# Dilated attention on one core: keys and values held whole, or loaded per pair of heads in a full-array layout

## The chip, the cores and the metric

The kernel runs on one core of one Trainium2 chip. The metric is the device time of one execution of the whole program, in microseconds (us). Times and traces come from the chip's own profiler.

## The reference

Two transformer blocks over 256 tokens of width 1024. The first block holds, in this order, feed-forward layers, a gated linear recurrence, shared keys and values, and a dilated attention. The part that the change touches is the last two:

```python
kv = (x @ kv_w).reshape(bsz, s, 2, N_HEADS, HEAD_DIM)      # 16 heads of 64
...
q = (x @ w_q).reshape(bsz, s, N_GROUPS, N_HEADS, HEAD_DIM) # three query groups
for g, (window, dilation) in enumerate(((128, 1), (512, 4), (2048, 16))):
    o, l = dilated_group(q[:, :, g], k, v, slopes, window, dilation)
...
wts = softmax(stack(lses), axis=0)
out = sum(wts[..., None] * stack(outs), axis=0)
return out.reshape(bsz, s, N_HEADS * HEAD_DIM) @ w_o
```

In `dilated_group` a query at t sees the keys t, t-d, t-2d, ... within its window, with a bias of minus slope times distance. Weighting three softmaxes by the softmax of their log-sum-exps is one softmax over the scores of the three groups side by side, and so the kernel computes it.

## The kernel before, in words

All large products are done in F32R, a float form with a shortened mantissa that TensorE takes in one pass. To keep accuracy each operand is split into a high and a low part, and three matmuls are summed (high by high, high by low, low by high; `mm3`). Weights stream from memory in units of eight 128x128 tiles: SyncE's queue brings a unit (`raw`), ScalarE rounds it to the high part (`whi`, L87), VectorE subtracts to get the low part (`wlo`, L99). `pump` keeps the splits up to six units ahead of use.

`kv` (the stage of shared keys and values) makes keys with features on partitions, two heads of 64 to a tile of 128, and writes their high and low parts to memory as `kh` and `kl`. Values have tokens on partitions and go to `vsc`, through `kt` (L634).

`attn` begins with seven loads on GpSimd's queue: the distance table `dt`, the scales `qs`, the keys `KH` (four loads, L653; each head's high part stands twice, in both halves of the partitions), `KL` (L654; low parts of two heads in the two halves), and the values `Vt` (L655). The queries are made by 24 tiles of matmuls in groups, `put` writes a head's high part into its own half of the partitions and the low part into the other half.

Heads go through a software pipeline, one `step` per head: `scores` of head i, `soft` of head i-1, `trans` of head i-2, `pv` of head i-3. The list `PLAN` says how many steps stand after each half group of query matmuls, `HOOKS` places the last ones amid the output projection's first wave. A scheduler then orders each engine's queue. In `scores` there are six products per head: for the later 128 queries and then for the earlier 128, each against the three groups. Each is two matmuls of 256 columns: the stacked high and low queries against KH (128 rows), and the high queries alone against KL (64 rows):

```python
self.mm(b[:, i], q[:, i % 3, c], KH[:, h, :], i % 2 == 0, False)
self.mm(b[:, i], q[r, i % 3, c], KL[r, pr, :], False, True)
```

VectorE adds the distances and takes the maximum in one instruction (L687 for the later queries, 768 columns, L690 for the earlier, 384), scales the maxima (`m`, L693), ScalarE takes exponentials with a running sum (L694, L695). In `soft` GpSimd adds two groups (L705), VectorE the third and the division (L706, L707). `trans` transposes on TensorE, ScalarE copies back (`pt`, L717). In `pv` the values of a head (64 columns of weights) are multiplied with `pt`; even heads fill the lower, odd heads the upper half of one PSUM bank's partitions. These products are in plain f32, which takes two instructions each in the trace.

Of the kernel before, what the change touches and what calls it, by code (L numbers as in the profile page):

```python
# [8 lines left out]
F32 = mybir.dt.float32  # L9
# [26 lines left out]
HOOKS = (1, 3, 5)  # L36
RAWS = 5
# [20 lines left out]
class Builder:  # L58
# [13 lines left out]
    # ---------------------------------------------------------------- weights  # L72
# [96 lines left out]
    # ---------------------------------------------------------------- layer norm  # L169
# [4 lines left out]
    def emb_begin(self):  # L174
        """The columns and the meta tokens that the norm of all tokens adds to the first block's last one."""
# [8 lines left out]
    def sums(self, m, N, off, sq, eng, eng2=None):  # L184
        """Running sums of x and x^2 over the feature tiles."""
# [32 lines left out]
    def prep(self, ms, ln, N, off, fold=True):  # L218
        """What the next norm needs of the feature tiles ms, which end together."""
# [24 lines left out]
    def scale_in(self, m, ln, N, off):  # L244
        """x <- x g, once the sums have what they need of it."""
# [9 lines left out]
    def stats(self, N, eps, tail=None, dst=None):  # L255
        """Mean and deviation of every token from the running sums; tail: the last tile's share comes on top."""
# [46 lines left out]
    def norm_last(self, ln, N, off, i, eng, rstd, nm):  # L303
        """Normalises a feature tile that scale_in has been over."""
# [17 lines left out]
    def filler(self, specs, ln, N, off, eps, pool, tag="fv", bufs=2, when=(1, 3)):  # L322
        """First output tiles of a stage, from the not yet normalised input."""
# [84 lines left out]
    def out_proj(self, K, hh, hl, spec, coef, ln, N, off, fold, waves, korder=None, hooks={}):  # L408
        """x <- x + coef * (h @ W), in waves of output tiles; hooks: what is emitted amid the first wave."""
# [22 lines left out]
    # ---------------------------------------------------------------- feed forward  # L432
# [26 lines left out]
    # ---------------------------------------------------------------- RG-LRU  # L459
# [142 lines left out]
    # ---------------------------------------------------------------- shared keys and values  # L602
    def kv(self, ln_in, eps):
        nc = self.nc
        N, off = SEQ, META
        with self.tc.tile_pool(name="kv", bufs=1) as p:
# [16 lines left out]
            for c in range(4):  # L623
# [9 lines left out]
                t = p.tile([128, 2, N], F32, tag="kt", name="kt", bufs=2)  # L633
                nc.scalar.copy(t, P)  # L634
                nc.scalar.dma_start(out=self.vsc[:, :, c * 256:(c + 1) * 256], in_=t)

    # ---------------------------------------------------------------- dilated attention
    def attn(self, ln_in, ln_out, eps):
        nc = self.nc
        N, off = SEQ, META  # L640
        with self.tc.tile_pool(name="attn", bufs=1) as p:
            KH = p.tile([128, N_HEADS, N], F32R, name="KH")
            KL = p.tile([128, 8, N], F32R, name="KL")
            Vt = p.tile([128, 2, D], F32, name="Vt")
# [17 lines left out]
            def put(pr, g, src):  # L662
                """High part of a head's queries in its own half of the partitions, low part in the other one."""
# [11 lines left out]
            def scores(h):  # L675
                e, pr = h % 2, h // 2
                q = Q[pr][e]
                r = slice(64 * e, 64 * e + 64)
                b = self.bank(3).rearrange("p a n -> p (a n)").rearrange("p (g n) -> p g n", n=N)
# [762 lines left out]
```

## Time and profile before

| | |
|---|---|
| median of 3 runs | 1812.07 us (1810.32 to 1812.13) |
| profiled execution, span from first to last instruction | 1813.3 us (the page gives no other time of its own) |
| TensorE (PE) busy | 1741.0 us, 96% |
| VectorE (DVE) busy | 1272.0 us, 70% |
| ScalarE (ACT) busy | 1032.6 us, 57% |
| GpSimd (POOL) busy | 230.0 us, 13% |
| mean granted TensorE clock | 0.970 |
| dilated attention, first score matmul to the end of the output projection's first wave | 772.3 to 938.3 us |

PE rows are matmuls, PEld rows the loads of their weights. A matmul's duration in a row includes the way through the array, so that neighbours overlap; what a matmul costs in a stream is the distance of its start from the next start. PEclk is the granted clock, as a share of 2.4 GHz.

### The profile page before, as it was taken

The page shows a single profiled execution, that of the slowest core. Times are in us where ns is not written, and L with a number is a line of the kernel's source. Part 1 is how long each engine was busy: PE and PEld are TensorE (multiplying, and loading weights), DVE is VectorE, ACT ScalarE, POOL GpSimd, SP SyncE. Part 2 cuts the span into 40 slices and gives each one's busy share as a digit, 9 for nine tenths or more (in the row PEclk, how much of TensorE's full clock was granted, in tenths as well). Part 3 has the DMA queues.
Part 4 walks back from the last instruction along what each step waited for, and adds up shares of the span by engine and source line. Part 5 has one row for each costly group of instructions (what it writes and reads, how often), then busy time and mean ns, then how long its engine had stood idle before and what let it go on. Part 6 is the DMA issues. An engine that isn't in the chain of part 4 may idle for free.

```text
span 1813.3 us, 34554 instructions
## 1 busy us (share of the span) xinstructions
PE 1741.0 (96%) x13558; PEld 1675.4 (92%) x13558; DVE 1272.0 (70%) x2399; ACT 1032.6 (57%) x2090; POOL 230.0 (13%) x266
## 2 busy tenths in 40 slices
PE   8999978999999999999999999799999999999997
PEld 8999977999999999977789999788999998899996
DVE  6666899966676666756668666897965569687653
ACT  6444666744465444644547445775744457575443
POOL 0001355000100001201120001320200030120001
PEclk9999988999999999968999999999999999999999
DMA  8555435565548555732225555433365554246550
GB/s 292 185 187 186 145 105 168 170 209 186 182 156 280 186 187 186 208 118 82 82 85 179 188 183 184 154 106 106 118 208 176 177 188 152 83 129 223 186 186 35
DMA packets 85372, 296.80 MB, mean 164 GB/s; under 512 B 10892, under 2 KB 14232, under 8 KB 84696
## 3 DMA queue, kind: packets, MB, share of 16 engines
q1 hardware_dynamic: 80216, 283.79, 47.1%
q0 software_dynamic: 1424, 7.38, 1.3%
q10 hardware_dynamic: 3568, 3.41, 0.6%
q8 instruction: 106, 1.74, 0.4%
q14 instruction: 58, 0.48, 0.1%
HBM read 290.24 MB, written 4.19 MB: 162 GB/s over the span
## 4 chain that ended last, share of the span: by engine, by line
PE 82%; DVE 11%; ACT 3%; issue 2%; DMA 1%; POOL 1%; DVEq 0%; SPq 0%; POOLq 0%; ACTq 0%
PE ps L147 81%; DVE wlo L99 3%; DMA KL<-kl 1%; PE ps L155 1%; ACT whi L87 1%; DVE uc L510 0%; DVE gl L300 0%; DVE T L561 0%; DVE xf L252 0%; POOL wlo L99 0%; DVE nt L291 0%; DVE gl L215 0%; POOL acc L193 0%; DVE rstd L277 0%; DMA raw<-in_wst_dram 0%
## 5 line engine op out<-in xcount | busy, mean ns | idle before, releaser
L87 ACT CAST whi<-raw 128x512 fp32r<-128x512 f32 x1074 | 615.5, 617 | 525.7 <-issue 311.0
L99 DVE TENSOR_TENSOR wlo<-raw,whi 128x512 fp32r<-128x512 f32 x1032 | 685.7, 701 | 321.5 <-ACT whi L87 319.6
L147 PE MATMUL ps<-gh,whi 128*128 128x256 f32 (+3 forms) x2864 | 829.0, 290 | 19.6 <-ACT gh L297 8.7
L147 PE MATMUL ps<-gl,whi 128*128 128x256 f32 (+3 forms) x2864 | 823.3, 288 | 1.0 <-DVE gl L300 1.0
L147 PE MATMUL ps<-gh,wlo 128*128 128x256 f32 (+3 forms) x2864 | 818.4, 286 | 0.0
L147 PEld LDWEIGHTS ps<-gh,whi 128*128 128x128 f32 x2864 | 549.3, 192 | 27.2 <-ACT gh L297 9.3
L147 PEld LDWEIGHTS ps<-gl,whi 128*128 128x128 f32 x2864 | 550.9, 192 | 5.9 <-issue 2.6
L147 PEld LDWEIGHTS ps<-gh,wlo 128*128 128x128 f32 x2864 | 551.1, 192 | 1.3 <-issue 0.7
L147 PE MATMUL ps<-hh,wlo 128*128 128x256 f32 (+1 forms) x1056 | 298.0, 282 | 0.0
L147 PE MATMUL ps<-hh,whi 128*128 128x256 f32 (+1 forms) x1056 | 297.9, 282 | 0.0
L147 PE MATMUL ps<-hl,whi 128*128 128x256 f32 (+1 forms) x1056 | 297.7, 282 | 0.0
L147 PEld LDWEIGHTS ps<-hl,whi 128*128 128x128 f32 x1056 | 199.0, 188 | 0.0
L147 PEld LDWEIGHTS ps<-hh,whi 128*128 128x128 f32 x1056 | 199.0, 188 | 0.0
L147 PEld LDWEIGHTS ps<-hh,wlo 128*128 128x128 f32 x1056 | 198.8, 188 | 0.0
L193 POOL TENSOR_TENSOR acc<-xf 128x256 f32<-128x256 f32 (+1 forms) x10 | 7.6, 759 | 1060.7 <-DVE xf L252 907.7
L443 DVE TENSOR_TENSOR th<-th,ps 128x512 f32<-128x512 f32 (+1 forms) x62 | 42.9, 691 | 54.3 <-PE ps L147 54.3
L193 POOL TENSOR_TENSOR acc<-acc,xf 128x256 f32<-128x256 f32 (+1 forms) x50 | 45.5, 910 | 192.3 <-DVE xf L252 177.3
L99 POOL TENSOR_TENSOR wlo<-raw,whi 128x512 fp32r<-128x512 f32 x42 | 63.3, 1536 | 46.2 <-ACT whi L87 46.2
L252 DVE SCALAR_TENSOR_TENSOR xf<-ps,xf 128x256 f32<-128x256 f32 (+1 forms) x80 | 32.9, 422 | 41.1 <-PE ps L147 40.9
L198 ACT ACTIVATE sq<-xf 128x256 f32<-128x256 f32 (+1 forms) x88 | 35.6, 410 | 44.6 <-DVE xf L252 36.8
L211 ACT ACTIVATE gh<-xf,prm 128x256 fp32r<-128x256 f32 (+1 forms) x64 | 32.1, 508 | 47.9 <-DVE xf L252 47.9
L215 DVE SCALAR_TENSOR_TENSOR gl<-xf,prm,gh 128x256 fp32r<-128x256 f32 (+1 forms) x64 | 44.5, 706 | 11.0 <-ACT gh L211 11.0
(330 smaller groups left out, 1927.8 us busy)
## 6 DMA issues: line engine op xcount, KB each, us to landing
raw<-in_wst_dram SPq DMA_DIRECT2D x537, 512.0 KB, 3.4
cst<-in_c_mix_dram POOLq DMA_DIRECT2D x2, 1138.0 KB, 5.5
KH<-kh POOLq DMA_DIRECT2D x4, 512.0 KB, 13.7
kh<-kh ACTq DMA_DIRECT2D x4, 256.0 KB, 4.8
kl<-kl ACTq DMA_DIRECT2D x4, 256.0 KB, 6.6
vsc<-kt ACTq DMA_DIRECT2D x4, 256.0 KB, 6.0
KL<-kl POOLq DMA_DIRECT2D x1, 1024.0 KB, 21.5
Vt<-vsc POOLq DMA_DIRECT2D x1, 1024.0 KB, 23.9
```

The lines of the kernel that those rows point to most:

```text
L87: self.nc.scalar.copy(hi[:, q:q + 512], self.raws[u][:, q:q + 512])
L99: eng.tensor_tensor(lo[:, q:q + 512], r[:, q:q + 512], h[:, q:q + 512], op=ALU.subtract)
L147: self.nc.tensor.matmul(out, lhsT, rhs, start=start, stop=stop, skip_group_check=True)
L155: self.nc.tensor.matmul(out, in_, self.ident[0:n, 0:n], start=True, stop=True, is_transpose=True, skip_group_check=True)
L193: eng.tensor_tensor(a[:, 0, 0:N], x0, x, op=ALU.add)
L198: self.nc.scalar.activation(sq[:, 0:N], self.xf[:, m, off:off + N], AF.Square)
L211: return self.nc.scalar.activation(self.gh[:, m, c], self.xf[:, m, off:off + N], AF.Copy, scale=g)
L215: return self.nc.vector.scalar_tensor_tensor(self.gl[:, m, c], self.xf[:, m, off:off + N], g, self.gh[:, m, c].bitcast(F32), op0=ALU.mult, ...
L252: self.nc.vector.scalar_tensor_tensor(x, banks[m][:, 0:N], coef, x, op0=ALU.mult, op1=ALU.add)
L443: nc.vector.tensor_tensor(th, th, pu, op=ALU.mult)
```

## The change

Keys go to memory as one array `khl` with high and low parts side by side, values as `vsc` with each head's 64 columns inside 128, the other 64 zero (two `kt` buffers zeroed once by GpSimd, filled by four small copies per 256 columns). Attention loads keys and values per pair of heads into five rotating buffers (`KVB`), the first pair before the table, the last three pairs as buffers come free. Both score matmuls of a product now contract over 128 rows: against high parts that stand in both halves, and against low parts that stand in both halves (so that low by low is added too). The earlier queries take 128 columns of keys in place of 256, and lie without gaps in PSUM. The slope is folded into the reduction (minimum in place of maximum), and the scaling of `m` goes. In `pv` both heads of a pair are summed into the whole bank, each with zeros in the other's half.

```diff
+KVB = 5
 def kv(self, ln_in, eps):
             def put(c2, src):
-                h = p.tile([128, 2, N], F32R, tag="kh", name="kh", bufs=2)
-                lo = p.tile([128, 2, N], F32R, tag="kl", name="kl", bufs=2)
-                self.split(h, lo, src)
-                nc.scalar.dma_start(out=self.kh[:, 2 * c2:2 * c2 + 2, :], in_=h.bitcast(F32))
-                nc.scalar.dma_start(out=self.kl[:, 2 * c2:2 * c2 + 2, :], in_=lo.bitcast(F32))
+                h = p.tile([128, 2, 2, N], F32R, tag="kh", name="kh", bufs=2)
+                self.split(h[:, :, 0], h[:, :, 1], src)
+                nc.scalar.dma_start(out=self.khl[:, 2 * c2:2 * c2 + 2], in_=h.bitcast(F32))
...
+            KT = [p.tile([128, 2, 2, 2, 128], F32, name="kt") for _ in range(2)]
+            for t in KT:
+                nc.gpsimd.memset(t, 0.0)
...
-                t = p.tile([128, 2, N], F32, tag="kt", name="kt", bufs=2)
-                nc.scalar.copy(t, P)
-                nc.scalar.dma_start(out=self.vsc[:, :, c * 256:(c + 1) * 256], in_=t)
+                t = KT[c % 2]
+                P = P.rearrange("p t (a e d) -> p a t e d", a=2, e=2)
+                for i in range(2):
+                    for e in range(2):
+                        nc.scalar.copy(t[:, i, :, e, 64 * e:64 * e + 64], P[:, i, :, e, :])
+                nc.scalar.dma_start(out=self.vsc[:, 2 * c:2 * c + 2], in_=t)
 def attn(self, ln_in, ln_out, eps):
+            def load(pr):
+                K = p.tile([128, 2, 2, N], F32R, tag="K", name="K", bufs=KVB)
+                W = p.tile([128, 2, 2, 128], F32, tag="W", name="W", bufs=KVB)
+                for e in range(2):
+                    for r in (0, 64):
+                        nc.gpsimd.dma_start(out=K[r:r + 64, e].bitcast(F32), in_=self.khl[64 * e:64 * e + 64, pr])
+                nc.gpsimd.dma_start(out=W, in_=self.vsc[:, pr])
+                KV[pr] = K, W
+            load(0)
...
-            for e in range(2):
-                for r in (0, 64):
-                    nc.gpsimd.dma_start(out=KH[r:r + 64, e::2, :].bitcast(F32), in_=self.kh[64 * e:64 * e + 64])
-            nc.gpsimd.dma_start(out=KL.bitcast(F32), in_=self.kl)
-            nc.gpsimd.dma_start(out=Vt, in_=self.vsc)
+            for pr in range(1, KVB):
+                load(pr)
...
                 for i in range(6):
-                    c = slice(128, 256) if i < 3 else slice(0, 128)
-                    self.mm(b[:, i], q[:, i % 3, c], KH[:, h, :], i % 2 == 0, False)
-                    self.mm(b[:, i], q[r, i % 3, c], KL[r, pr, :], False, True)
+                    c, n, o = (slice(128, 256), 256, i * 256) if i < 3 else (slice(0, 128), 128, 384 + i * 128)
+                    for t in range(2):
+                        self.mm(b[:, o:o + n], q[:, i % 3, c], K[:, e, t, 0:n], o % 512 == 0 and t == 0, t == 1)
...
-                nc.vector.tensor_scalar(m, m, -SLOPES[h], None, op0=ALU.mult)
...
             def pv(h):
-                self.mm(b[r:r + 64, 0:256], Vt[:, 0, h * 64:(h + 1) * 64], pt[:, 0:256], True, False)
-                self.mm(b[r:r + 64, 128:256], Vt[:, 1, h * 64:(h + 1) * 64], pt[:, 256:384], False, True)
-                if h % 2:
+                self.mm(b[:, 0:256], W[:, 0, e], pt[:, 0:256], e == 0, False)
+                self.mm(b[:, 128:256], W[:, 1, e], pt[:, 256:384], False, e == 1)
+                if e:
                     del self.held["o"]
-                    self.split(oh[:, h // 2], ol[:, h // 2], b[:, 0:256])
+                    self.split(oh[:, pr], ol[:, pr], b[:, 0:256])
+                    if pr + KVB < 8:
+                        load(pr + KVB)
```

The order of the queues moves with it. TensorE around the first score matmuls of a late head, before (`gh`, `gl` are the normalised input's parts, `q` the queries):

```order
L147 MATMUL ps<-KH,q 128x256
L147 MATMUL ps<-KL,q 128x256
L147 MATMUL ps<-KH,q 128x256
L147 MATMUL ps<-KL,q 128x256
L147 MATMUL ps<-gh,whi 128x256
L147 MATMUL ps<-gl,whi 128x256
L147 MATMUL ps<-gh,wlo 128x256
```

and a late head after the change, with the transposes of one head and the value products of another behind it:

```order
L148 MATMUL ps<-K,q 128x256 x6
L148 MATMUL ps<-K,q 128x128 x8
L148 MATMUL ps<-gh,whi 128x256
L156 MATMUL ps<-ident,t 128x128 x3
L148 MATMUL ps<-pt,W 128x256
L148 MATMUL ps<-pt,W 128x128
```

KH and KL no longer alternate, and half of the score matmuls have 128 columns. At the very start of attention's scores, 4 score matmuls, 4 weight matmuls, 4 score matmuls, 24 weight matmuls and 2 score matmuls stand ahead of the first reduction.

GpSimd's queue at the start of attention, before:

```order
L649 DMA dt<-in_c_dist_dram 128x1152
L650 DMA qs<-in_c_qs_dram 128x8
L653 DMA KH<-kh 64x8x256 x4
L654 DMA KL<-kl 128x2048
L655 DMA Vt<-vsc 128x2048
L705 TENSOR_TENSOR t<-s 128x256
L705 TENSOR_TENSOR t<-s 128x128
```

and after, from the last of the first five pairs on (`K` and `W` are a pair's keys and values):

```order
L657 DMA W<-vsc 128x512
L656 DMA K<-khl 64x512
L712 TENSOR_TENSOR t<-s 128x256
L656 DMA K<-khl 64x512
L712 TENSOR_TENSOR t<-s 128x128
L656 DMA K<-khl 64x512
L712 TENSOR_TENSOR t<-s 128x256
L712 TENSOR_TENSOR t<-s 128x128
L656 DMA K<-khl 64x512
```

The loads of the sixth pair stand between the additions of the first two heads; each waits until its part of a buffer has been read.

## Rows read from the trace of the kernel before

**Rows 1.** The page's shares of the span: engine, busy us, instructions.
```profile
PE 1741.0 (96%) x13558; PEld 1675.4 (92%) x13558; DVE 1272.0 (70%) x2399; ACT 1032.6 (57%) x2090; POOL 230.0 (13%) x266
```

**Rows 2.** Busy time by stretch: PE, PEld, DVE, ACT, POOL, granted clock, DMA.
```profile
772.30:938.30 166.00, 162.35 (x809) 124.79 (x808) 101.98 (x250) 77.77 (x167) 21.62 (x32) 0.85 0.26 86
```

**Rows 3.** TensorE's timeline at the full clock, then its weight loads: start, us, what.
```profile
902.64 0.28 PE L147 MATMUL ps<-gh,wlo 128*128 128x256 f32 x1
902.76 0.28 PE L147 MATMUL ps<-KH,q 128*128 128x256 f32 x1
902.97 0.38 PE L147 MATMUL ps<-KL,q 64*128 64x256 f32 x1
903.28 0.38 PE L147 MATMUL ps<-KH,q 128*128 128x256 f32 x1
...
902.64 0.19 PEld L147 LDWEIGHTS ps<-KH,q 128*128 128x128 f32 x1
902.97 0.18 PEld L147 LDWEIGHTS ps<-KL,q 64*128 64x128 f32 x1
```

**Rows 4.** TensorE's timeline at the lower clock level.
```profile
796.89 0.58 PE L147 MATMUL ps<-KL,q 64*128 64x256 f32 x1
797.40 0.58 PE L147 MATMUL ps<-gh,whi 128*128 128x256 f32 x1
797.77 0.41 PE L147 MATMUL ps<-gl,whi 128*128 128x256 f32 x1
797.99 0.41 PE L147 MATMUL ps<-gh,wlo 128*128 128x256 f32 x1
```

**Rows 5.** TensorE's waits in the stretch: us in total, times, longest.
```profile
PE ps L147 <- DMA KL<-kl: 3.6, 1, 3.6
```

**Rows 6.** Busy time by shorter stretches, columns as in rows 2.
```profile
778.30:801.50 23.20, 23.20 (x78) 17.30 (x78) 10.39 (x24) 7.73 (x18) 2.68 (x4) 0.57 0.19 67
...
808.00:828.00 20.00, 20.00 (x84) 16.18 (x83) 10.68 (x30) 7.69 (x18) 2.31 (x4) 0.66 0.17 54
```

**Rows 7.** Groups of instructions in the stretch: TensorE's score matmuls on KL.
```profile
L147 PE MATMUL ps<-KL,q 64*128 64x256 f32 x96 | 40.0, 417 | 3.6 <-DMA KL<-kl 3.6
```

**Rows 8.** TensorE's timeline in the second block: plain f32 products on the full array.
```profile
1243.21 0.41 PE L147 MATMUL ps<-Qr,Kr 128*128 128x128 f32 x2
1243.46 0.81 PE L147 MATMUL ps<-Vr,st 128*128 128x96 f32 x6
1244.10 0.84 PE L147 MATMUL ps<-Qr,Kr 128*128 128x256 f32 x4
1244.78 0.81 PE L147 MATMUL ps<-Vr,st 128*128 128x96 f32 x6
```

**Rows 9.** TensorE's timeline: the value products of one head, and what follows.
```profile
906.89 0.86 PE L147 MATMUL ps<-pt,Vt 128*64 128x256 f32 x4
907.69 0.38 PE L147 MATMUL ps<-gh,whi 128*128 128x256 f32 x1
```

**Rows 10.** Weight loads of 64 and of 128 columns: ns minimum, median, maximum.
```profile
L147 PEld LDWEIGHTS ps<-pt,Vt x64: 132/137/231, 809.3 to 935.8; 128*64 128x64 f32 x64
...
L147 PEld LDWEIGHTS ps<-Qr,Kr x32: 188/190/192, 1235.5 to 1570.2; 128*128 128x128 f32 x32
```

**Rows 11.** GpSimd's groups from 740 to 940: the issues of KH.
```profile
L653 POOL DMA_DIRECT2D KH<-kh x4 | 2.8, 695 | 0.0
```

**Rows 12.** VectorE's groups in the stretch: the scaling of m.
```profile
L693 DVE TENSOR_SCALAR m<-m 128x2 f32<-128x2 f32 x16 | 2.6, 164 | 0.2
```

**Rows 13.** The tile kt in the keys-and-values stage: ns minimum, median, maximum.
```profile
L634 ACT COPY kt<-ps x4: 577/580/588, 550.7 to 563.6; 128x512 f32<-128x512 f32 x4
```

**Rows 14.** Busy time in the second block's two mixers, columns as in rows 2.
```profile
1190.00:1290.00 100.00, 93.35 (x656) 83.24 (x655) 82.93 (x216) 65.41 (x166) 23.95 (x32) 0.97 0.34 112
1495.00:1595.00 100.00, 96.03 (x703) 88.48 (x702) 79.81 (x209) 65.70 (x169) 10.83 (x21) 0.98 0.38 127
```

**Rows 15.** VectorE's timeline: the first reduction of the softmax.
```profile
788.46 0.96 DVE L687 CUSTOM_DVE_ANT_0 s<-ps,dt 128x768 f32<-128x768 f32 x1 [6.72 <-PE ps L147]
```

More of the change, by code (lines that the diff above doesn't have):

```diff
@@ L641, in attn @@
         with self.tc.tile_pool(name="attn", bufs=1) as p:
-            KH = p.tile([128, N_HEADS, N], F32R, name="KH")
-            KL = p.tile([128, 8, N], F32R, name="KL")
-            Vt = p.tile([128, 2, D], F32, name="Vt")
+            KV = {}
+            def load(pr):
[7 more added lines that the diff above has]
+            load(0)
             dt = p.tile([128, 1152], F32, name="dt")
@@ L676, in scores @@
                 e, pr = h % 2, h // 2
-                q = Q[pr][e]
-                r = slice(64 * e, 64 * e + 64)
-                b = self.bank(3).rearrange("p a n -> p (a n)").rearrange("p (g n) -> p g n", n=N)
+                q, K = Q[pr][e], KV[pr][0]
+                b = self.bank(3).rearrange("p a n -> p (a n)")
                 for i in range(6):
-                    c = slice(128, 256) if i < 3 else slice(0, 128)
-                    self.mm(b[:, i], q[:, i % 3, c], KH[:, h, :], i % 2 == 0, False)
-                    self.mm(b[:, i], q[r, i % 3, c], KL[r, pr, :], False, True)
+                    c, n, o = (slice(128, 256), 256, i * 256) if i < 3 else (slice(0, 128), 128, 384 + i * 128)
+                    for t in range(2):
+                        self.mm(b[:, o:o + n], q[:, i % 3, c], K[:, e, t, 0:n], o % 512 == 0 and t == 0, t == 1)
                 s = p.tile([128, 1152], F32, tag="s", name="s", bufs=2)
@@ L686, in scores @@
                 den = p.tile([128, 2], F32, tag="den", name="den", bufs=3)
-                nc.vector.tensor_tensor_reduce(out=s[:, 0:768].rearrange("p (g n) -> p g n", g=3), in0=b[:, 0:3],
-                                               in1=dt[:, 0:768].rearrange("p (g n) -> p g n", g=3), scale=1.0, scalar=-3e38,
-                                               op0=ALU.add, op1=ALU.max, accum_out=m[:, 0:1])
-                nc.vector.tensor_tensor_reduce(out=s[:, 768:1152].rearrange("p (g n) -> p g n", g=3), in0=b[:, 3:6, 0:128],
-                                               in1=dt[:, 768:1152].rearrange("p (g n) -> p g n", g=3), scale=1.0,
-                                               scalar=-3e38, op0=ALU.add, op1=ALU.max, accum_out=m[:, 1:2])
-                nc.vector.tensor_scalar(m, m, -SLOPES[h], None, op0=ALU.mult)
-                nc.scalar.activation(s[:, 0:768], s[:, 0:768], AF.Exp, scale=SLOPES[h], bias=m[:, 0:1], accum_out=den[:, 0:1])
-                nc.scalar.activation(s[:, 768:1152], s[:, 768:1152], AF.Exp, scale=SLOPES[h], bias=m[:, 1:2],
-                                     accum_out=den[:, 1:2])
+                for j, (a, z) in enumerate(((0, 768), (768, 1152))):
+                    nc.vector.tensor_tensor_reduce(out=s[:, a:z], in0=b[:, a:z], in1=dt[:, a:z], scale=-SLOPES[h], scalar=3e38,
+                                                   op0=ALU.add, op1=ALU.min, accum_out=m[:, j:j + 1])
+                for j, (a, z) in enumerate(((0, 768), (768, 1152))):
+                    nc.scalar.activation(s[:, a:z], s[:, a:z], AF.Exp, scale=-1.0, bias=m[:, j:j + 1], accum_out=den[:, j:j + 1])
                 S[h], DEN[h] = s, den
@@ L721, in pv @@
                 pt = PT.pop(h)
-                r = 64 * (h % 2)
-                if h % 2 == 0:
-                    O[h // 2] = self.bank(hold="o")
-                b = O[h // 2]
-                self.mm(b[r:r + 64, 0:256], Vt[:, 0, h * 64:(h + 1) * 64], pt[:, 0:256], True, False)
-                self.mm(b[r:r + 64, 128:256], Vt[:, 1, h * 64:(h + 1) * 64], pt[:, 256:384], False, True)
-                if h % 2:
+                pr, e = h // 2, h % 2
+                if e == 0:
+                    O[pr] = self.bank(hold="o")
+                b, W = O[pr], KV[pr][1]
+                self.mm(b[:, 0:256], W[:, 0, e], pt[:, 0:256], e == 0, False)
+                self.mm(b[:, 128:256], W[:, 1, e], pt[:, 256:384], False, e == 1)
+                if e:
                     del self.held["o"]
-                    self.split(oh[:, h // 2], ol[:, h // 2], b[:, 0:256])
+                    self.split(oh[:, pr], ol[:, pr], b[:, 0:256])
+                    if pr + KVB < 8:
+                        load(pr + KVB)
             steps = iter(range(N_HEADS + 3))
@@ L1219, in build @@
             self.ps = pp.tile([128, 8, 512], F32, name="ps")
-            self.kh = pd.tile([128, 8, SEQ], F32, name="kh")
-            self.kl = pd.tile([128, 8, SEQ], F32, name="kl")
-            self.vsc = pd.tile([128, 2, D], F32, name="vsc")
+            self.khl = pd.tile([128, 8, 2, SEQ], F32, name="khl")
+            self.vsc = pd.tile([128, 8, 2, 2, 128], F32, name="vsc")
             self.xf = cp.tile([128, KD, LTOT], F32, name="xf")
```

## The prediction

> **What bounds the kernel now.** The page's share table comes first: TensorE is busy 96% of the span [rows 1], so a gain has to come off its queue. The part-by-part view of the trace, cut to the stretch from the first score matmul to the last matmul of the output projection's first wave, comes next. It lasts 166 us; VectorE is busy 102 us of it, TensorE 162 us at a granted clock of 0.85 [rows 2]. So TensorE ends this stretch too, but it is busy in a poor way, and its timeline shows how. Two weight matmuls stand 0.12 us apart (902.64 to 902.76), at 256 columns each. As soon as a score matmul on 64 rows (KL) alternates with one on 128 rows (KH), starts are 0.31 us apart (902.97 to 903.28) with the same 256 columns [rows 3]. At the lower clock level the pair is 0.51 against 0.22 [rows 4]. The loads tell why: the load for the KH matmul that follows a weight matmul starts at 902.64, beside the matmul before it, but the load for KL starts at 902.97 together with its own matmul, and so on from there [rows 3]. I read this as the change of array shape between neighbours, since the 64-row operand is what sets them apart from the weight matmuls.
>
> Two more losses lie in the same stretch. TensorE stands 3.6 us for the transfer of KL [rows 5]. And the clock falls: 0.85 over 166 us, between levels of 1.2 and 2.4 GHz, means (1 - 0.85) x 2 x 166 = 50 us at the lower level, of which half, 25 us, is lost. It falls after that stand and in long runs of score matmuls: 0.57 in the 23 us from 778, 0.66 in the 20 us from 808 [rows 6].
>
> **The change, part by part.** The one stretch that I cost is that of 166 us; all sums are against the profiled span of 1813.3 us. The median of the three runs is 1.2 us below, and I take 1.2 off at the end.
>
> *Scores.* 96 matmuls on KL [rows 7] and as many on KH become 192 of 128 rows each; 96 keep 256 columns, 96 (the earlier queries, which see half of the keys) go to 128. Before, 192 x 0.31 = 59.5 us at the full clock. The 256-column ones become what the weight matmuls are: 96 x 0.12 = 11.5 us. For the 128-column ones the trace has no row: every one-pass (F32R) matmul in it has 256 columns or more. From below, half of a 256-column one, 0.06; from above, a plain f32 product of 128 columns, which takes two instructions, 0.25 from 1243.21 to 1243.46 [rows 8]. I take 0.12: a single instruction of that f32 pair costs 0.125, and a one-pass instruction of twice the columns costs 0.12, so both neighbours agree. That is 11.5 us, ends 6 and 24. Scores save 59.5 - 23 = 36.5 us (24 to 42).
>
> *Values.* The two products of a head now have 128 output columns in the weights (half of them zero) and the same moving columns. Before: 0.80 us per head, 906.89 to 907.69 [rows 9]. The same four instructions on the full array exist in the second block: 1244.10 to 1244.78, 0.68 us [rows 8]. So 16 x 0.12 = 1.9 us saved. Against this: a load of 64 columns takes 137 ns, one of 128 takes 190 ns [rows 10], so 64 loads are 64 x 0.053 = 3.4 us longer. The row of 0.68 has such loads inside, so I count them as hidden; if they were bare, the term would be +3.4 instead of -1.9, and this end goes into the range. The Trainium skill, "TensorE: Matmul & The Clock Gate", section "LDWEIGHTS (loading the stationary operand)", says that the time of a load follows its columns and not its rows, which speaks against widening 64 to 128; by it the term would be the +3.4, by the row of 0.68 it is not.
>
> *Transfers.* One pair's keys and values (768 KB) are asked for first, then the rest, in 25 + 2 issues where there were 7. At 0.695 us each [rows 11] GpSimd is done issuing some 19 us after 751, so by 770; the first pair is issued after 3.5 us, and its data are needed at 772. The 3.6 us stand goes. The last three pairs' 15 issues stand among GpSimd's additions for the softmax, 15 x 0.7 = 10.4 us on an engine with 21.6 us of work in 166 [rows 2]. Behind a waiting issue stands the next head's addition, and VectorE's next addition waits for that. The issues wait for score or value products of earlier heads, which come before the addition's own input in TensorE's order. I cost them at nothing; if each group of four delayed the chain by its 2.8 us, three pairs cost 8 us.
>
> *VectorE and ScalarE.* 16 small multiplications of m go, 164 ns each [rows 12]: 2.6 us off VectorE, 102 to 99.4. The two reductions keep their sizes. In the keys-and-values stage ScalarE makes 16 copies of 128 columns in place of 4 of 512 (580 ns each [rows 13]): between nothing and 12 x 0.58 = 7 us more, beside TensorE; the view of that tile names nobody who waited for the copies, so on the path I take 0. GpSimd's two memsets stand alone in its queue there: 0.
>
> **The sum.** TensorE's work in the stretch, at the full clock and without the stand, is 166 - 3.6 - 25 = 137.4 us; less 36.5 and 1.9 it is 99 us (93 to 117). That is as much as VectorE's 99.4, so neither will run without gaps. The nearest picture of such a mix is the second block's mixers, 100 us each: TensorE busy 94.7% on average, clock 0.975, VectorE busy 81% [rows 14]. By TensorE's share the stretch takes 99 / (0.947 x 0.975) = 107 us; by VectorE's share 99.4 / 0.814 = 122 us. Between the two I take 117, where VectorE is at 85%. The gain is 166 - 117 = 49 us: 1813.3 - 49 - 1.2 = **1763 us**. What is late next is VectorE: its share of weight splitting and the softmax of the next head. My likeliest case spans 107 to 126 us for the stretch, 1753 to 1772.
>
> **The rivals.**
> *VectorE does not bind (0.15).* Its splits can run ahead of need into the following stage; then TensorE alone sets 98 to 107 us, 1744 to 1753. For it: the splits are done several units ahead. Against it: VectorE is 81% busy where the mixers already make TensorE wait.
> *Narrow matmuls are dear (0.20).* At 0.25 us and above, TensorE has 112 us or more, over 0.923 at least 121, with VectorE's gaps 122 to 140: 1768 to 1786. Nothing in the trace excludes it, as the narrow one-pass form is not there.
> *The array shape is not the cause (0.06).* If the loads stay bare because the score weights are freshly written queries, starts stay at 0.31 us and only the stand and a part of the clock return: a stretch of 150 to 162 us, 1796 to 1808; the lower third of this chance lies within 0.2% of before. Against it: the KH matmul that follows a weight matmul at 902.76 has no gap before it, though its weights are queries too.
> *Slower: the clock stays down (0.03).* TensorE would now wait for VectorE in many short pieces, and if that holds the clock at 1.2 GHz for the whole stretch, 93 to 117 us of work become 186 to 234, so 20 to 68 us more than 166: 1832 to 1880. It decides from the point where 99 / (1 - f/2) = 166, a share f of 0.81 at the lower level; before, f was 50 / 166 = 0.30, and in the mixers 0.05. The Trainium skill, "TensorE: Matmul & The Clock Gate", section "A second HAM failure mode: psum-queue depth-cycling", describes this pattern of small waits between groups that bring the slow clock back; the mixers' 0.975, with such waits, speaks against it here.
>
> **How the numbers follow.** My own case has 0.56, at 1763. The range must leave out no more than 0.2: it takes the whole of my case, the narrow-matmul case, and the near half of the case in which VectorE does not bind: 1747 to 1788. About 0.2% (3.6 us) is what a measurement here can tell from no change. Slower has 0.03; the part of the third rival near before gives 0.02 to no change; faster has 0.95.
>
> **What would show it.** In the trace after: score matmuls of 256 columns 0.12 us apart at the full clock (step one right), the 128-column ones 0.12 (0.25 or more: the second rival); a head's value products 0.68 us long; no wait of TensorE for K or W; the first reduction of the softmax near 777 (38 matmuls of 0.12 us after 772.3, by the order), where it started at 788.46 before [rows 15]; VectorE at 80 to 90% of the stretch, and TensorE waiting for it a few times; granted clock over 0.95. A clock under 0.85 in the stretch, starts still 0.31 apart, or GpSimd's additions waiting for transfers would make me wrong.

## The result, and the profile after

The changed kernel takes 1770.05 us (median of 4 runs, 1765.08 to 1770.94), the kernel before, beside it, 1811.19 us (4 runs, 1805.56 to 1812.13). The ratio is 0.9778, 95% interval 0.9757 to 0.9799: about 41 us less, and inside the range forecast. The profiled execution has a span of 1769.2 us.

First the page's shares, to be read beside [rows 1]:

```profile
PE 1687.3 (95%) x13558; PEld 1654.5 (94%) x13558; DVE 1268.4 (72%) x2383; ACT 1031.7 (58%) x2102; POOL 247.8 (14%) x302
```

TensorE has as many instructions as before and is busy 54 us less. Next the busy time by stretch, columns as in [rows 2]: the whole stretch from the first score matmul to the end of the output projection's first wave, then two pieces of its start.

```profile
772.30:893.90 121.60, 108.14 (x808) 103.75 (x807) 99.06 (x233) 76.50 (x166) 30.13 (x52) 0.93 0.45 135
...
772.30:784.70 12.40, 8.02 (x58) 7.23 (x57) 8.70 (x16) 8.14 (x17) 2.93 (x6) 0.85 0.92 247
784.70:792.00 7.30, 7.27 (x36) 7.30 (x37) 6.98 (x15) 3.41 (x10) 3.86 (x7) 0.55 0.38 102
```

The stretch begins at the same 772.3 us and lasts 121.6 us where it lasted 166: 44.4 us less, the whole difference between the two profiled spans (44.1). VectorE is busy 99.06 us (99.4 forecast), 81% of it. TensorE now stands for 13.4 us. TensorE's waits in the stretch (us in total, times, longest), to be read beside [rows 5]:

```profile
PE ps L148 <- DVE q L681: 5.9, 9, 1.3
PE ps L156 <- DVE q L681: 3.1, 1, 3.1
PE ps L148 <- DVE m L700: 2.8, 2, 2.2
```

No row names keys or values: the 3.6 us for KL are gone, and every large wait is for VectorE. 9.0 of the 13.4 us end with L681, where VectorE makes the low parts of the queries from PSUM; L700 is a reduction of the softmax. The longest wait, of six transposes, with the work of VectorE ahead of it:

```profile
802.45 0.55 DVE L714 TENSOR_SCALAR t<-t,den 128x256 f32<-128x256 f32 x2
802.91 0.68 DVE L100 TENSOR_TENSOR wlo<-raw,whi 128x512 fp32r<-128x512 f32 x1
803.63 0.49 DVE L681 SCALAR_TENSOR_TENSOR q<-ps,qs,q 64x256 fp32r<-64x256 f32 x1
804.17 0.33 PE L156 MATMUL ps<-ident,t 128*128 128x128 f32 x1 [3.06 <-DVE q L681]
```

The last divisions (L714) that the transposes need end at 803.00, yet the transposes start only at 804.17, 0.05 us behind L681, whose result they do not read. That they wait for the PSUM space that L681 reads from is likely and not tested.

TensorE's timeline at the full clock, beside [rows 3] and [rows 9]:

```profile
794.77 1.48 PE L148 MATMUL ps<-K,q 128*128 128x256 f32 x12
796.09 0.87 PE L148 MATMUL ps<-pt,W 128*128 128x256 f32 x4
796.72 0.37 PE L148 MATMUL ps<-gh,whi 128*128 128x256 f32 x1
```

The twelve score matmuls of a head take 796.09 - 794.77 = 1.32 us, 0.11 each, where neighbours stood 0.31 apart; with 0.12 for the six of 256 columns, those of 128 take 0.10. A head's value products take 0.63 us, before 0.80.

The low clock from 784.7 to 792 us was not forecast. Just ahead of it the weights come late; in all engines' waits from 768 to 800:

```profile
ACT whi L88 <- DMA raw<-in_wst_dram: 4.2, 2, 2.8
```

### The profile page after: what moved, and what is told of

Read it like the earlier page. It is cut to its first block, busy times and chain, and to the rows that moved or that the text cites. A ratio compares the mean times of both kernels' runs of the same rounds, so it can differ in the third digit from the quotient of the medians.

```text
span 1769.2 us, 34606 instructions
## 1 busy us (share of the span) xinstructions
PE 1687.3 (95%) x13558; PEld 1654.5 (94%) x13558; DVE 1268.4 (72%) x2383; ACT 1031.7 (58%) x2102; POOL 247.8 (14%) x302
## 3 DMA queue, kind: packets, MB, share of 16 engines
q10 hardware_dynamic: 2480, 4.46, 0.8%
## 4 chain that ended last, share of the span: by engine, by line
PE 78%; DVE 14%; ACT 3%; issue 2%; POOL 1%; DMA 1%; DVEq 0%; SPq 0%; ACTq 0%; POOLq 0%
PE ps L148 78%; DVE wlo L100 3%; ACT whi L88 1%; DMA raw<-in_wst_dram 1%; PE ps L156 1%; DVE q L681 1%; DVE s L700 1%; DVE uc L511 0%; DVE gl L301 0%; DVE xf L253 0%; DVE T L562 0%; POOL wlo L100 0%; DVE nt L292 0%; DVE fv L320 0%; DVE gl L216 0%
## 5 line engine op out<-in xcount | busy, mean ns | idle before, releaser
L216 DVE SCALAR_TENSOR_TENSOR gl<-xf,prm,gh 128x256 fp32r<-128x256 f32 (+1 forms) x64 | 44.4, 705 | 11.1 <-ACT gh L212 11.1
```

The costliest lines, as they stand in the source:

```text
L216: return self.nc.vector.scalar_tensor_tensor(self.gl[:, m, c], self.xf[:, m, off:off + N], g, self.gh[:, m, c].bitcast(F32), op0=ALU.mult, ...
```

## The experiments

All ratios are to the kernel before on the same chip. The runs e1 to e4 and e13 shared one chip, e5 to e12 another, so between those two groups the ratios are compared and not the times. Diffs are against the changed kernel unless said otherwise. "Wide" is a kernel with 256 key columns for all queries, "narrow" one with 128 for the earlier queries.

| run | edit | median us (range) | ratio (95%) |
|---|---|---|---|
| e1_low64 | low keys on 64 rows again | 1786.63 (1785.11 to 1792.49) | 0.989 (0.9871 to 0.991) |
| e2_pv64 | value weights 64 columns again | 1766.77 (1765.24 to 1768.06) | 0.9776 (0.9761 to 0.9791) |
| e3_cols256 | 256 key columns for all queries | 1760.26 (1759.04 to 1761.55) | 0.9738 (0.9723 to 0.9754) |
| e4_bufs3 | three buffers | 1765.04 (1761.59 to 1765.23) | 0.976 (0.9744 to 0.9776) |
| e5_after_again | none | 1767.98 (1764.57 to 1769.59) | 0.9773 (0.9751 to 0.9794) |
| e9_cols128_gaps | 128 columns, 256 apart | 1765.77 (1764.81 to 1768.12) | 0.9764 (0.9744 to 0.9783) |
| e7_actdiv | division on ScalarE | 1770.75 (1770.53 to 1773.99) | 0.9793 (0.9773 to 0.9814) |
| e8_before_dtlate | before, table asked for last | 1807.67 (1803.38 to 1812.14) | 0.9991 (0.9976 to 1.0006) |
| e10_plan | PLAN | 1767.41 (1766.18 to 1768.95) | 0.9771 (0.9751 to 0.9792) |
| e11_256_b3 | 256 columns, three buffers | 1759.66 (1759.45 to 1760.04) | 0.9728 (0.9705 to 0.9751) |
| e12_plan_b3 | PLAN, three buffers | 1764.39 (1761.83 to 1765.48) | 0.9754 (0.9731 to 0.9777) |
| e13_lopool | e11 with splits on GpSimd | 1764.96 (1761.99 to 1767.42) | 0.9761 (0.9731 to 0.9792) |

**Is it the array shape?**

```diff
-                    for t in range(2):
-                        self.mm(b[:, o:o + n], q[:, i % 3, c], K[:, e, t, 0:n], o % 512 == 0 and t == 0, t == 1)
+                    r = slice(64 * e, 64 * e + 64)
+                    self.mm(b[:, o:o + n], q[:, i % 3, c], K[:, e, 0, 0:n], o % 512 == 0, False)
+                    self.mm(b[:, o:o + n], q[r, i % 3, c], K[r, e, 1, 0:n], False, True)
```

> The changed kernel with one thing undone: the score matmul on the low parts of the keys contracts over 64 rows again (the low-by-low product is left out), everything else as changed. If the change of array shape between neighbours is what kept weight loads bare, starts of score matmuls are 0.31 us apart again for 256 columns and about 0.26 for 128, so about 3.4 us per head in place of 1.32: 33 us more TensorE work, of which the 13 us of TensorE's idle time in the stretch take a part, and the clock falls below 0.90 there. The stretch goes from 121.6 to 145 to 160 us, the time to 1790 to 1808 us. Rival (the loads were bare because the queries are freshly written, and the gain came from the transfers and the clock): starts stay at 0.12 and the time within 3 us of 1770.

Half of the gain goes, from 0.978 to 0.989. The time is a little under the 1790 to 1808 us expected. TensorE's timeline in this run: a run of 27 score products at the start, a head at the full clock, a product of 64 rows with its load, and the first of the head's products of 128 columns:

```profile
777.66 9.28 PE L148 MATMUL ps<-K,q 128*128 128x256 f32 x27
...
795.68 3.38 PE L148 MATMUL ps<-K,q 128*128 128x256 f32 x12
798.98 1.41 PE L148 MATMUL ps<-pt,W 128*128 128x256 f32 x3
...
795.88 0.38 PE L148 MATMUL ps<-K,q 64*128 64x256 f32 x1
795.88 0.18 PEld L148 LDWEIGHTS ps<-K,q 64*128 64x128 f32 x1
...
797.45 0.33 PE L148 MATMUL ps<-K,q 128*128 128x128 f32 x1
```

Its busy time by stretch, the whole and two pieces of the start:

```profile
772.30:915.90 143.60, 143.54 (x805) 121.38 (x805) 99.29 (x233) 76.41 (x164) 30.62 (x52) 0.88 0.36 114
...
777.70:786.70 9.00, 9.00 (x29) 5.82 (x28) 7.00 (x18) 5.97 (x14) 3.93 (x8) 0.74 0.66 202
786.70:792.00 5.30, 5.30 (x25) 5.17 (x25) 3.27 (x6) 0.01 (x1) 0.43 (x1) 0.50 0.57 167
```

Twelve products now take 798.98 - 795.68 = 3.30 us, with nothing else changed: 0.275 each against 0.11. The load of a 64-row product starts together with its product (795.88), as before the change. So alternating 64 and 128 rows is what bares the loads. The Trainium skill, "TensorEngine Tiling (Array Packing)", section "Key Properties", says that a change of the tiling mode drains TensorE; this run fits that and gives the price, some 0.17 us per matmul. And the stretch is full of TensorE again, without a wait of note (143.54 of 143.60 us). In the two pieces TensorE never stands, yet in the run of 27 such score matmuls the granted clock is 0.74, and for the 5.3 us behind it 0.50. So the slow form goes with two losses, its gaps and a low clock.

**Are wide value weights worth anything?** Products on 64 weight columns as before, each head into its half of the partitions.

```diff
-                self.mm(b[:, 0:256], W[:, 0, e], pt[:, 0:256], e == 0, False)
+                self.mm(b[r, 0:256], W[:, 0, e, r], pt[:, 0:256], True, False)
...
```

> The changed kernel with the value products on 64 weight columns again, each head into its own half of the partitions. Theory: a head's products go from 0.63 back to 0.80 us and the matmul behind them starts bare, so about 0.2 x 16 = 3 us more TensorE work, but TensorE idles 13 us in the stretch waiting for VectorE, so the time rises by 0 to 3 us (1770 to 1773). Rival (loads cost by their columns): 64 loads of 137 in place of 190 ns, the time falls by up to 3.4 us.

The same time as the changed kernel within the interval, though in its trace a head's value products take 0.79 us again (792.36 to 793.15) in place of 0.63. The term of -1.9 us can't be seen in the time, nor the other end of +3.4; TensorE has 13 us of waits in which such a term can vanish.

**Are narrow score products worth anything?** All products with 256 columns, 256 apart in PSUM; the unused halves of the earlier queries are computed and not read.

```diff
-                    c, n, o = (slice(128, 256), 256, i * 256) if i < 3 else (slice(0, 128), 128, 384 + i * 128)
+                    c, n, o = slice(128, 256) if i < 3 else slice(0, 128), 256, i * 256
...
```

> The changed kernel with all score matmuls at 256 columns (half of the earlier queries' columns unused, as before the change). Theory: a one-pass matmul of 128 columns costs 0.10 us and one of 256 0.12, so a head's scores go from 1.32 to 1.43 us, 2 us more TensorE work in the stretch and 0 to 2 us in the time. Rival (fewer columns are what the gain comes from): each of 96 matmuls costs 0.05 us more and the time rises by 5 us or more.

Both theories miss: more work, and less time, 0.9738. Busy time in this run; its first score product starts at 773.48, so the stretch itself lasts 112.5 us:

```profile
772.30:886.00 113.70, 105.26 (x817) 99.45 (x816) 100.62 (x235) 77.62 (x168) 34.28 (x54) 1.00 0.49 147
```

The clock is 1.00 all through. The runs further down look for the reason. (The lines left out of the diff let VectorE read the columns where they now lie.)

**Do the transfers disturb the weights?** Three buffers in place of five:

```diff
-KVB = 5
+KVB = 3
```

> The changed kernel with three buffers of keys and values in place of five: 2.3 MB of them asked for at the start, in place of 3.8. Theory: the weight units that came late at 774 to 782 (ScalarE waited 4.2 us for them) were late because of this burst; with three buffers that wait goes, TensorE's 4.4 us idle before 785 and the low clock until 791 go with it, and the time falls by 3 to 8 us, to 1762 to 1767. Rival (VectorE's own queue, the splits of the queries and the first reductions, sets that piece): the wait for weights goes but the time stays within 2 us of 1770; if later loads are now late, TensorE waits for K somewhere and the time rises.

0.976, its interval across that of the changed kernel: at most some 3 us. In its trace ScalarE waits for no weights from 768 to 800, as expected. But the low clock did not go with that wait:

```profile
772.30:784.70 12.40, 11.29 (x65) 10.57 (x64) 12.01 (x25) 8.68 (x20) 4.39 (x8) 0.73 0.56 170
780.00:784.70 4.70, 4.70 (x23) 4.70 (x23) 4.62 (x11) 1.63 (x5) 2.80 (x6) 0.50 0.36 94
```

So late weights are not needed for the low clock there, and taken alone this run settles little.

**The same kernel again, and the layout apart from the columns.**

> The changed kernel as it is, on the same chip as the three kernels beside it, so that differences of a few us can be read. Expected: ratio to the kernel before 0.978 (0.976 to 0.980). Whether the low clock of 7 us near 785 us in the trace is a fixed part of this kernel (it comes again, at most 0.60 in some 7 us before 795) or an accident of one execution (it does not come) is what the trace is to show; after an accident the span would be 1760 to 1765, as in the runs with three buffers.

0.9773. In this execution the low clock near 785 us does not come, ScalarE waits 1.1 us for weights in place of 4.2, and the span is 1762.9 us, 6.3 less. Its first score product starts at 770.15. The stretch from there, then a later piece:

```profile
770.15:887.80 117.65, 105.09 (x807) 100.44 (x807) 99.04 (x233) 76.35 (x166) 28.28 (x48) 0.97 0.42 138
...
792.00:812.00 20.00, 16.98 (x126) 16.32 (x126) 18.96 (x45) 12.38 (x27) 6.58 (x12) 0.91 0.56 179
```

So the very late weights and the low clock at 785 us together are an accident that some executions of the same kernel have. It is worth 4 us, 121.6 against 117.7. The other 2.2 us between the two spans lie ahead of the stretch; they are there already 281 us into the execution.

```diff
-                    c, n, o = (slice(128, 256), 256, i * 256) if i < 3 else (slice(0, 128), 128, 384 + i * 128)
+                    c, n, o = (slice(128, 256), 256, i * 256) if i < 3 else (slice(0, 128), 128, i * 256)
...
```

> The earlier queries' products keep 128 key columns, but lie in PSUM 256 columns apart, as in the kernel before, in place of side by side; so those of the first two groups no longer share their bank with the third group's start, and TensorE's order becomes six score products, then weights, where it was four. It separates the two things that the run with 256 columns changed at once. Theory layout: the 6 us that 256 columns gained came from the order that the layout gives; then this kernel is as fast or faster than that one, ratio 0.971 to 0.975, and the first reduction of the softmax or the score products before it are earlier. Theory columns: the narrow products themselves cost more than they save; then this kernel stays at 0.977 to 0.980, as the changed kernel. Theory accident: all differ by chance of the clock, and the changed kernel beside it lies at 0.974 too.

0.9764, between the two expectations, and the changed kernel beside it is not at 0.974, which speaks against chance alone. The layout alone does not bring all that 256 columns bring, though this interval and that of the wide kernel overlap by 0.001.

**Does VectorE's total bind?**

```diff
-                    nc.vector.tensor_scalar(o, o, den[:, i:i + 1], None, op0=ALU.mult)
+                    nc.scalar.activation(o, o, AF.Copy, scale=den[:, i:i + 1])
```

> The 32 multiplications by the reciprocal sum move from VectorE to ScalarE (some 11.7 us less on VectorE in the attention stretch, more on ScalarE, which is 63% busy there). Theory of the prediction: VectorE binds beside TensorE and sets the gaps; with 99 us reduced to 88, TensorE's idle time of 13.4 us in the stretch falls by some 4 to 10 us, ratio 0.972 to 0.976. Rival: TensorE's gaps come only at the start, from late weights and queries, before any division is done; then no difference from the changed kernel, within 2 us, or up to 4 us slower where ScalarE's exponentials come later.

0.9793: no gain, within what the rival allowed. VectorE's total over the stretch, taken alone, is not the bound. The test says less of the softmax of one head: the division is still in it, on ScalarE. And the longest wait of the transposes here (2.4 us) again ends with L681, as in the changed kernel. (This execution also has the accident near 785 us, so its waits are not compared.)

**What is the stand for KL worth, by itself?** Against the kernel before, from ahead of the loads of KH to behind that of KL:

```diff
-            nc.gpsimd.dma_start(out=dt, in_=self.ins["c_dist"])
...
+            nc.gpsimd.dma_start(out=dt, in_=self.ins["c_dist"])
```

> The kernel before with one edit: the distance table is asked for after the low keys in place of ahead of the high keys, so that the low keys land earlier. It measures what the stand of TensorE for the low keys (3.6 us) is worth with the drop of the clock that follows it. Theory: the stand goes, and the low clock of the first 23 us behind it (0.57, some 8 us lost) partly with it; 4 to 10 us faster, ratio 0.994 to 0.998. Rival: another transfer, of the table or of the weights, is late in its place, and long runs of score products pull the clock down anyway; no difference, 0.998 to 1.002.

No difference. But the test is weak: TensorE still stands 2.3 us, now ahead of the first score product, which starts at 776.65 where it started at 772.67 before. The trace shows why: a weight unit is late for ScalarE, and the queries, which come behind it, are late too:

```profile
773.21 0.62 ACT L87 CAST whi<-raw 128x512 fp32r<-128x512 f32 x1 [2.26 <-DMA raw<-in_wst_dram]
775.06 1.46 ACT L667 ACTIVATE q<-fv,qs 64x512 fp32r<-64x512 f32 x2
775.81 1.53 DVE L668 SCALAR_TENSOR_TENSOR q<-fv,qs,q 64x512 fp32r<-64x512 f32 x2 [2.11 <-ACT q L667]
776.65 0.36 PE L147 MATMUL ps<-KH,q 128*128 128x256 f32 x1 [2.30 <-issue]
```

So the first part of the rival came true, another transfer late in the place of the low keys. What a start without any stand is worth stays open.

**Is it one place in TensorE's order?** In the second execution of the changed kernel, after twelve score products at 793.49, TensorE waits 3.02 us for transposes, and the value products behind them run at half the clock. The expectation calls this a wait for the softmax; it ends at 798.00 behind L681 (797.45 to 797.94), 1.2 us after that head's divisions.

```diff
-PLAN = (1, 1, 0, 1, 1, 1, 1, 1, 0, 1, 1, 1, 1, 0, 1, 0, 1, 1, 2)
+PLAN = (1, 1, 0, 1, 1, 0, 1, 1, 1, 1, 1, 1, 1, 0, 1, 0, 1, 1, 2)
```

> One entry of the list PLAN moves: the half group of query matmuls without a step comes fifth in place of eighth. All score products stay as in the changed kernel, 128 columns and side by side. It takes away one place in TensorE's order, the six transposes of two heads straight behind a run of 12 score products, at which the changed kernel waits 3.0 us for the softmax of the second head and then runs at 1.2 GHz. Theory order: the 256-column kernel was faster because its order does not have this place; then this kernel, with narrow products, gains too: no wait over 2 us in 790 to 800 us, granted clock over 0.95 there, ratio 0.973 to 0.976. Theory columns: narrow products are what costs; then 0.977 to 0.979 as the changed kernel.

0.9771: the theory of order falls in this form. The wait only moved; 2.5 us of it are still there, at 802.81 (this execution has the accident too). With three buffers on top, once wide (the edit of e3_cols256) and once narrow with the moved entry:

```diff
-KVB = 5
+KVB = 3
```

> Two edits together: 256 key columns for all queries and three key buffers in place of five. If the later transfers and the order of TensorE are two separate losses, the gains add up: the 256-column kernel's 0.9738 less some 0.001, ratio 0.9715 to 0.9735. If both only remove the same low clock near 785 us, it stays at 0.9735 to 0.975.

> The moved entry of PLAN and three key buffers, narrow products. If the theory order holds and the losses add up, ratio 0.972 to 0.975, no slower than 256 columns with three buffers by more than 0.001; if narrow products cost by themselves, 0.976 to 0.979.

0.9728, as if the gains added up, though it can't be told from the wide kernel with five buffers (0.9738); and 0.9754, between its two expectations. On this chip the wide kernel's slowest run (1760.04) is below the narrow one's fastest (1761.83). TensorE's timeline, first of the narrow kernel with three buffers, then of the wide one: rows that wait, and what follows.

```profile
797.69 0.55 PE L156 MATMUL ps<-ident,t 128*128 128x128 f32 x3 [2.48 <-DVE q L681]
799.02 2.51 PE L148 MATMUL ps<-K,q 128*128 128x256 f32 x12
```

```profile
792.97 0.74 PE L148 MATMUL ps<-K,q 128*128 128x256 f32 x4 [0.20 <-DVE q L681]
793.97 0.74 PE L148 MATMUL ps<-K,q 128*128 128x256 f32 x4 [0.26 <-DVE m L702]
797.34 0.55 PE L156 MATMUL ps<-ident,t 128*128 128x128 f32 x3 [1.32 <-DVE t L716]
799.07 0.55 PE L156 MATMUL ps<-ident,t 128*128 128x128 f32 x3
```

And the busy time around that place, narrow, then wide:

```profile
792.00:812.00 20.00, 17.52 (x135) 17.15 (x134) 19.14 (x47) 13.61 (x29) 7.76 (x13) 0.91 0.62 185
```

```profile
772.00:800.00 28.00, 25.16 (x196) 23.48 (x194) 27.25 (x59) 19.97 (x44) 10.59 (x16) 1.00 0.50 156
792.00:812.00 20.00, 18.23 (x139) 16.72 (x138) 19.51 (x52) 14.53 (x32) 8.22 (x14) 1.00 0.52 160
```

In both, VectorE has next to no gap there (19.14 and 19.51 of 20.00 us). What differs around this place is how TensorE waits for it. The narrow kernel stands 2.5 us at one go, until L681 ends, and the twelve score products behind the stand take 2.3 us (to the next transposes, at 801.34) in place of 1.3. The wide one waits in pieces of 0.2 to 1.3 us, the longest for a division (L716), with score products between them, and its clock stays at 1.00. Over the whole stretch, each from its own first score product, narrow and then wide:

```profile
770.33:886.70 116.37, 104.29 (x807) 99.21 (x807) 101.06 (x232) 76.76 (x166) 33.84 (x57) 0.99 0.46 143
771.30:883.15 111.85, 104.19 (x807) 98.28 (x807) 100.09 (x233) 76.56 (x166) 36.07 (x57) 1.00 0.47 149
```

TensorE is busy equally long in both; nearly all of the 4.5 us is that it stands less in the wide kernel, 7.7 us in place of 12.1. So the columns that narrowing saves (96 x 0.02 = 1.9 us) are lost again to a low clock and to waits, and the way in which the waits are cut up is not the main thing: their sum is. Whether the shorter waits come from the wider products themselves or from the order that the scheduler makes of them stays open: no narrow kernel was run in the wide one's order.

**Would less work on VectorE in that window help?**

```diff
+LO_POOL = (259, 261, 263)
...
-        eng = self.nc.gpsimd if pool or self.lo_pool else self.nc.vector
+        eng = self.nc.gpsimd if pool or self.lo_pool or u in LO_POOL else self.nc.vector
```

> The kernel with 256 columns and three buffers, and of the weight units that VectorE splits between about 772 and 800 us three (259, 261, 263) have their low parts made by GpSimd: six pieces, 6 x 0.69 = 4.1 us off VectorE where it runs without a gap from 772 to 800 us, 6 x 1.48 = 8.9 us onto GpSimd. Theory: in this window, and in it alone, VectorE is the bound, so TensorE's waits there shrink by some 2 to 4 us; ratio 0.970 to 0.972, VectorE idle for over 1 us between 772 and 800. Rival: the chain of one head's softmax is the bound (GpSimd's addition stands in it), not VectorE's total, and GpSimd's additions now stand behind its splits; no gain, or 1 to 5 us slower, 0.973 to 0.976.

Slower than the kernel that it was made from, 0.9761 against 0.9728 (the intervals overlap, and the chips differ; on its own chip all its times, 1761.99 us and up, lie above the wide kernel's with five buffers, 1759.04 to 1761.55). Timelines of VectorE, GpSimd and TensorE in this run:

```profile
785.35 4.46 DVE L717 TENSOR_SCALAR t<-t,den 128x256 f32<-128x256 f32 x2
...
786.10 1.17 POOL L715 TENSOR_TENSOR t<-s 128x256 f32<-128x256 f32 x2
787.23 2.49 POOL L101 TENSOR_TENSOR wlo<-raw,whi 128x512 fp32r<-128x512 f32 x2
...
792.76 0.90 PE L157 MATMUL ps<-ident,t 128*128 128x128 f32 x3 [4.73 <-DVE q L682]
```

Two divisions, 0.54 us elsewhere in this run (794.70), take 4.46 us: they end at 789.81, when GpSimd's splits end (789.72). TensorE then stands 4.73 us before that head's transposes, a stand that ends not with the divisions but with L682 (the queries), held up behind them on VectorE. The expectation's rival was right in the outcome, though not in the way: it is not GpSimd's additions that were late, but VectorE that stood while GpSimd worked. TensorE's order came out otherwise too in this kernel, so the whole difference can't be put down to the two divisions.

## Why the prediction was right

- **Bound and cause.** Right. Putting back the 64-row products alone gives back half of the gain (e1_low64), and the spacing with them.
- **Scores.** 23 us forecast for 192 matmuls; 16 heads at 1.32 us are 21.1 us. The 128-column product, for which no row stood before, takes 0.10 us (0.12 taken, ends 0.06 and 0.25): the rival "narrow matmuls are dear" is out. The trace of before held a nearer neighbour than the two ends, shown below.
- **Values.** 0.63 us a head (0.68 forecast), loads hidden, as taken. In the time the term does not show: e2_pv64 differs by nothing that can be measured.
- **TensorE's work.** 99 us forecast at the full clock. In the execution without the accident it is busy 105.09 us at a clock of 0.97, so about 102 us.
- **The stretch.** 117 us forecast, from a mix of TensorE's share and VectorE's share in the mixers. Measured 117.7 us in the undisturbed execution and 121.6 in the other. The mix was no mechanism: 117 was picked between 107 and 122, and the upper end took VectorE's total for a bound, so meeting 117.7 is partly luck. VectorE at 81 to 84% (80 to 90 forecast). The first reduction stands at 776.95 us in the undisturbed execution (777 forecast) and 780.24 in the other, but the match is luck: score products began at 770.15 and 772.36, so it came 6.8 and 7.9 us behind the first of them, not 4.7.
- **The time.** 1763 us forecast, 1770.05 measured. The stretch accounts for 4.6 us of the 7. The rest is mostly the step from span to time: I took 1.2 off, and the changed kernel's times lie above their spans (1770.94 against 1769.2).
- **Late next: VectorE.** Right for the engine, by TensorE's waits, and wrong for its work: I named weight splitting and the softmax, but 9.0 of the 13.4 us end with the low parts of the queries (L681), and 3.6 with the reductions of the softmax. It is wrong too if read as VectorE's total alone, since taking the divisions off it brought nothing (e7_actdiv). The rival "VectorE does not bind" is out as well: TensorE stands 13 us.
- **Transfers at nothing.** This is the term that was mis-sized. I priced the issues on GpSimd's queue (27 of them, where eight stood before, not seven), and there nothing was nearly right: only the fifth head's additions were held up by waiting issues, starting 1.0 us behind their exponentials in place of 0.2 to 0.5. I missed the weights that come in the same moment. In all eight traces with five buffers ScalarE waits for a weight unit between 768 and 800 us, from 0.2 to 4.2 us in total, and in none of the four with three buffers. How much time that costs is shown less well: the accident is worth 4 us, but the low clock in it came without late weights too (e4_bufs3). Nor do busy DMA engines decide it alone: they are 92% busy from 772.3 to 784.7 us here and in e3_cols256, which waits 1.0 us and keeps its clock. The 4 us stay within the 0 to 8 us that I had kept, for another reason.
- **The zeroing at nothing.** GpSimd's second zeroing of `kt` comes only at 565.3 us and ScalarE stands 4.5 us for it. TensorE is busy for all of 550 to 600 us, so on the path the nothing held.
- **The clock.** Over 0.95 was forecast; it was 0.93 and 0.97. That narrow columns would cost some of the gain by longer stands was not among my cases.

The nearer neighbour of the narrow products, in TensorE's timeline before: three transposes, each a single instruction of 128 columns on the full array, and what follows them. They take 878.07 - 877.80 = 0.27 us, 0.09 each. A transpose is not such a product, but with this row the chance of 0.25 and above would have been smaller.

```profile
877.80 0.51 PE L155 MATMUL ps<-ident,t 128*128 128x128 f32 x3
878.07 0.36 PE L147 MATMUL ps<-gl,whi 128*128 128x256 f32 x1
```

The best version run has 256 columns and three buffers: 1759.66 us, 0.9728 of before (0.9705 to 0.9751), against 0.9778 for the change as it stands. Half of what the change gains is the array shape with its clock. The other half I did not take apart, and its cause is argued only: the stand for KL, 3.6 us by its row, the clock of the first 60 us (0.72 before, 0.89 after), and the narrow products as long as their loads are bare. With bare loads in e1_low64 the six of 128 columns take 798.98 - 797.45 = 1.53 us, 0.26 each where 256 columns stand 0.31 apart, so 96 of them save an estimated 5 us; with the loads hidden, narrowing gained nothing (e3_cols256).

## What to carry to other kernels

Look at the spacing of starts, not at busy time: TensorE was busy for 162 of 166 us by its records while score products of two array shapes stood 0.31 us apart, and 0.11 was possible in one shape. Bringing them to one shape paid although it added zeros and products. Once TensorE waits for another engine, shaving its columns need not save time: here the kernel with more columns was faster, and TensorE stood less in all. And price the transfers that a change pulls together on the DMA engines as well as on the queue that issues them, with the next user of those engines in view.

## What the hardware showed that I had not expected

- The clock falls without any wait. In e1_low64 TensorE is busy for all of 9.0 us, nearly all of it with matmuls of two shapes, and the granted clock is 0.74 there, then 0.50 over the next 5.3 us.
- A VectorE division on SBUF data (0.54 us for the pair) took 4.46 us beside GpSimd's splits and additions. The Trainium skill, "SBUF — State Buffer", section "Who interferes with whom", describes a port pair that VectorE and GpSimd share and that one of them holds alone; the trace agrees in that the divisions end within 0.1 us of GpSimd's last split. The wait spans four GpSimd instructions in a row, two additions and two splits (786.10 to 789.72). That the shared ports held it up is read from these times; no run tested it.
